# Attention scores of a diffusion step: three products over 64 rows become two products over 128 rows

## The chip, the cores and the metric

The kernel runs on one core of one Trainium2 chip. What is compared is device time in microseconds (us) of one execution of the whole program. The engines in the profile are PE (TensorE, the matmuls), PEld (the weight loads of TensorE, which overlap PE), DVE (VectorE), ACT (ScalarE), POOL (GpSimd) and SP (which here issues most DMAs).

## The reference, cut to what matters

One inference step of a two-layer backbone: layer 0 mixes tokens with a state-space scan, layer 1 with differential attention, and each is followed by a convolutional feed-forward block (FFN). There are 512 latent tokens ("sample") and 128 context tokens ("prompt"), width 1024. The change is in layer 1's attention only: 8 heads, and for each head two key maps of 64 dimensions.

```python
def diff_attend(q, k, v, lam):                       # q: b, lq, heads, 2 maps, 64
    def one_block(qi):                               # 128 queries
        s = jnp.einsum('bqhcd,bkhcd->bhcqk', qi, k) * DA_SCALE
        p = jax.nn.softmax(s, axis=-1)
        w = p[:, :, 0] - lam * p[:, :, 1]
        return jnp.einsum('bhqk,bkhd->bqhd', w, v)
    ...
qs, ks_ = rope_2d(qs, tabs), rope_2d(ks_, tabs)
k_all = jnp.concatenate([cache_k, ks_], axis=1)      # 128 cached + 512 own keys = 640
os_ = diff_out(diff_attend(qs, k_all, v_all, lam), ...)
op = diff_out(diff_attend(qp, kp, vp, lam), ...)     # the prompt sees its own 128 keys only
```

## The kernel before, in words

Activations are kept transposed: 128 channels on the partitions, 640 tokens (512 sample, 128 prompt) along the free dimension. A matmul in full precision is made of three products of `float32r` operands, each operand being split into a high part and a low part (`hi`, `lo`): hi*hi + hi*lo + lo*hi. `float32r` matmuls, weight tile by weight tile, are the dense work (tiles named q, k, v, po, up, ba, bb and so on).

A head's 128 channels hold both key maps: rows 0 to 63 are map 0, rows 64 to 127 are map 1. `attention` (L1299) loops over 8 heads. For each head it runs a q tile and a k tile on PE (8 steps of 6 matmuls each), copies them out of PSUM (`att_evac`, L1168), applies the rotary positions on DVE and splits into high and low parts (`att_q`, L1184: tiles `qh`, `ql`; `att_k`, L1193: `kh`, `kl`, 640 keys), and then adds the generator `att_head` (L1203) as a task. The v tile of the head follows. Tasks are advanced by `hook`, called after every dense step, so that the scores of head h are issued among the dense steps of head h+1; a "tick" is one dense step of six matmuls.

`att_head` first does the prompt (tile `sp`, plain float32, 128 queries by 128 keys, one matmul per map over that map's 64 rows; operands `qp`, `kp`). Then come four blocks b = 0 to 3 of 128 queries. A block takes two PSUM buffers (`sl`, one per map, from the pool `psd` of three buffers, which the dense tiles share), and fills them with 12 matmuls of 64 rows by 320 columns:

```python
for j, (x, kk) in enumerate(((qh, kh), (qh, kl), (ql, kh))):
    for c0 in (0, 320):
        for r, hf in zip(rs, half):      # map 0: rows 0-63, map 1: rows 64-127
            self.mm(r[...], x[hf, qb], kk[hf, c0:c0 + 320], j == 0, j == 2)
```

`softmax` follows for each map: a maximum on DVE (`sm<-sl`, L1212) and an exponential with row sums on ACT (`e<-sl`, L1213), which is the last reader of the PSUM buffer. Two ticks later `combine` makes the weights w of the block. When all four are done, `att_tail` (L1253) transposes the weights (`wt`, five groups of four float32 transposes through the one PSUM bank "m"), splits each group on ACT and DVE (`wTh`, `wTl`) and multiplies with v (`ov`). So the tail of head h-1, the scores of head h and the dense tiles of head h+1 are interleaved on PE.

The order on each engine is set by the framework's scheduler, which knows the order of the program, the dependencies and costs of its own; each engine then runs its own list strictly in order. The scores in the trace from 1062 to 1077 us are head 0's, 1090 to 1113 head 1's, 1131 to 1150 head 2's, then heads 3 to 6 at intervals of about 37.3 us, and 1308 to 1334 head 7's, among the matmuls of the output projection (`po`).

Of the kernel before, what the change touches and what calls it, by code (L numbers as in the profile page):

```python
# [18 lines left out]
P = 128  # L19
D = 1024  # L20
KT = D // P
TP = 128
TS = 512
T = TP + TS
# [3 lines left out]
PO = 256  # L28
# [5 lines left out]
NH = 32  # L34
FH = 2816
FT = FH // P
SUB = (((0, 8), (8, 15), (15, 22)), ((0, 7), (7, 14), (14, 22)))
MID = (9, 8)
DA_SCALE = 64 ** -0.5
# [128 lines left out]
class Step:  # L168
# [539 lines left out]
    def ffn(self, l, h, nextnorm, pool):  # L708
        nc = self.nc
        cw = pool.tile([P, 2 * FT, 4], F32, tag="fcw", name=f"fcw{l}", bufs=1)  # L710
        nc.sync.dma_start(cw, self.a["fcw"][l])
# [40 lines left out]
        blk = Blocks(self, h, epilogue, place)  # L752
        t = cw[:, FT + std:, 0:3]
        nc.vector.tensor_scalar(t, t, -1.0, None, ALU.mult)
        sums = None
        self.start_tiles(h)
        self.weight_sums(l, range(11, 14, SUMS) if l else range(std, FT, SUMS), h[0][0])
        done = 0
        sub = SUB[l]
        for s, (k0, k1) in enumerate(sub):  # L760
            last = s == len(sub) - 1
            self.down = False
            end = min(k1 + 1, FT)
            while done < end:
# [357 lines left out]
    def att_consts(self, pool):  # L1122
        nc, a = self.nc, self.a
        t = lambda shape, name, dt=F32: pool.tile(shape, dt, tag=name, name=name, bufs=1)
        self.rope = t([P, 2, TS], "rope")
        nc.sync.dma_start(self.rope, a["rope"])
        lv = t([P, 256], "lv")
        nc.sync.dma_start(lv, a["lam"])
        ls = t([P, 2], "ls")
        lj = t([P, 64], "lj")  # L1130
        for i in range(2):
            nc.vector.tensor_tensor_reduce(lj, lv[:, 128 * i:128 * i + 64], lv[:, 128 * i + 64:128 * i + 128], 1.0, 0.0,
                                           ALU.mult, ALU.add, ls[:, i:i + 1])
# [34 lines left out]
    def att_evac(self, ps, hd, name, pool):  # L1168

        x = self.slot("f", f"{name}{hd}", bufs=NF)[:, :TS]  # L1170
        p = pool.tile([P, TP], F32, tag=f"{name}p", name=f"{name}p{hd}", bufs=2)
        self.act(x, ps[:, PO:PO + TS], AF.Copy)
        self.act(p, ps[:, PO + TS:PO + T], AF.Copy, scale=DA_SCALE if name == "q" else 1.0)
        return x, p

    def att_rope(self, out, x):
# [7 lines left out]
    def att_q(self, x, hd, pool):  # L1184

        q = self.tmp("q")[:, :TS]
        self.att_rope(q, x)
        hi, lo = (pool.tile([P, TS], F32R, tag=f"q{nm}", name=f"q{nm}_{hd}", bufs=2) for nm in "hl")
        self.act(hi, q, AF.Copy, scale=DA_SCALE)
        self.stt(lo, q, DA_SCALE, hi.bitcast(F32), ALU.mult, ALU.subtract)  # L1190
        return hi, lo

    def att_k(self, x, hd, pool):  # L1193

        k = self.tmp("k")
        self.nc.sync.dma_start(k[:, TS:], self.a["ck"][hd])
        self.att_rope(k[:, :TS], x)
        hi, lo = (pool.tile([P, T], F32R, tag=f"k{nm}", name=f"k{nm}_{hd}", bufs=2) for nm in "hl")
        self.act(hi, k, AF.Copy)
        self.tt(lo, k, hi.bitcast(F32), ALU.subtract)  # L1200
        return hi, lo

    def att_head(self, hd, qp, kp, qs, k, vs, o, pool):  # L1203


        nc = self.nc
        (qh, ql), (kh, kl) = qs, k
        half = [slice(64 * m, 64 * m + 64) for m in range(2)]
# [17 lines left out]
        for m, hf in enumerate(half):  # L1226
            self.mm(r[:, 512 * m:512 * m + TP], qp[hf], kp[hf], True, True)
        st = stats()
        em = [softmax(r[:, 512 * m:512 * m + TP], TP, m, st) for m in range(2)]
        yield 2  # L1230
        last = hd == 7
        w = pool.tile([P, TP], F32, tag="wp", name="wp", bufs=1)
        combine(w, TP, *em, st)
        yield 3 if last else 4
        ws = []
        for b in range(4):
            qb = slice(b * P, (b + 1) * P)
            rs = [self.psd.tile([P, 1024], F32, tag="d", name="sl") for _ in range(2)]
            for j, (x, kk) in enumerate(((qh, kh), (qh, kl), (ql, kh))):
                for c0 in (0, 320):  # L1240
                    for r, hf in zip(rs, half):
                        self.mm(r[:, 192 + c0:192 + c0 + 320], x[hf, qb], kk[hf, c0:c0 + 320], j == 0, j == 2)
            st = stats()
            em = [softmax(r[:, 192:832], T, m, st) for m, r in enumerate(rs)]
            yield 2
            wb = pool.tile([P, T], F32, tag="w", name=f"w{b}", bufs=8)
            combine(wb, T, *em, st)
            ws.append(wb)
            if b < 3:
                yield ((1, 1, 1) if last else (1, 3, 1) if hd else (1, 3, 3))[b]  # L1250
        self.tails[hd] = self.add(self.att_tail(hd, w, ws, vs, o, pool), 1 if last else 2)
# [89 lines left out]
    def weight_units(self):  # L1341
# [10 lines left out]
        def ffn(l):  # L1352
# [10 lines left out]
            out = []  # L1363
            for k0, k1 in SUB[l]:
                end = min(k1 + 1, FT)
# [185 lines left out]
```

## Time and profile before

| what | value |
|---|---|
| time, median of 3 runs | 1862.02 us (1861.01 to 1862.44) |
| the profiled execution itself | 1865.19 us |
| its span, first to last instruction | 1863.4 us |
| busy PE / PEld / DVE / ACT | 1830.9 (98%) / 1715.6 (92%) / 1464.3 (79%) / 998.1 us (54%) |
| mean granted TensorE clock | 0.994 |
| attention stage, first q copy to last head's output | about 1049 to 1359 us |

The span is the time between the first and the last instruction; the 1.8 us around it are launch and end. A group of the profile is a line, an engine, an operation and tile names "out<-in", with shapes as partitions x elements. In a timeline a row is a start, a duration and a run of equal instructions (xN). Matmuls overlap in the pipeline, so a matmul's own duration (0.30 us for 320 columns) is longer than the time until the next may start; what a matmul costs is read from the distance between starts. Some matmul records can be missing.

### The profile page before, as it was taken

The page shows a single profiled execution, that of the slowest core. Times are in us where ns is not written, and L with a number is a line of the kernel's source. Part 1 is how long each engine was busy: PE and PEld are TensorE (multiplying, and loading weights), DVE is VectorE, ACT ScalarE, POOL GpSimd, SP SyncE. Part 2 cuts the span into 40 slices and gives each one's busy share as a digit, 9 for nine tenths or more (in the row PEclk, how much of TensorE's full clock was granted, in tenths as well). Part 3 has the DMA queues.
Part 4 walks back from the last instruction along what each step waited for, and adds up shares of the span by engine and source line. Part 5 has one row for each costly group of instructions (what it writes and reads, how often), then busy time and mean ns, then how long its engine had stood idle before and what let it go on. Part 6 is the DMA issues. An engine that isn't in the chain of part 4 may idle for free.

```text
span 1863.4 us, 33068 instructions
## 1 busy us (share of the span) xinstructions
PE 1830.9 (98%) x13057; PEld 1715.6 (92%) x13057; DVE 1464.3 (79%) x2827; ACT 998.1 (54%) x1862; POOL 55.7 (3%) x84
## 2 busy tenths in 40 slices
PE   7999999999999999999999999999999999999997
PEld 5899999999989999999999988888899999999996
DVE  5689999999848999998586877778779874874874
ACT  3379686879426442244363566566546543643641
POOL 0000000000001100011000000000001011100000
PEclk9999999999999999999999999999999999999998
DMA  9734244445547976677642211111047368853421
GB/s 339 270 108 147 92 126 128 114 132 177 184 148 220 279 217 211 208 205 201 208 133 77 88 46 59 57 52 49 21 129 193 95 180 237 250 166 103 142 80 57
DMA packets 108675, 276.06 MB, mean 148 GB/s; under 512 B 12284, under 2 KB 19048, under 8 KB 102504
## 3 DMA queue, kind: packets, MB, share of 16 engines
q1 hardware_dynamic: 100520, 225.19, 37.4%
q0 software_dynamic: 7424, 48.24, 11.0%
q8 instruction: 102, 1.67, 0.4%
q10 hardware_dynamic: 576, 0.52, 0.1%
q14 instruction: 53, 0.43, 0.1%
HBM read 267.95 MB, written 54.19 MB: 173 GB/s over the span
## 4 chain that ended last, share of the span: by engine, by line
PE 93%; DVE 3%; ACT 2%; DMA 1%; issue 1%; SPq 0%; DVEq 0%; ACTq 0%
PE po L230 25%; PE up L230 14%; PE bb L230 6%; PE ba L230 6%; PE bc L230 6%; PE z L230 6%; PE x L230 5%; PE st L230 5%; PE v L230 3%; PE yp L230 3%; PE q L230 2%; PE sl L230 2%; PE k L230 2%; PE ov L230 2%; PE in L230 1%; PE wt L1275 1%
## 5 line engine op out<-in xcount | busy, mean ns | idle before, releaser
L221 ACT ACTIVATE whi<-raw 128x1024 fp32r<-128x1024 f32 (+4 forms) x266 | 270.9, 1020 | 318.8 <-PE po L230 189.9
L227 DVE TENSOR_TENSOR wlo<-raw,whi 128x1024 fp32r<-128x1024 f32 (+4 forms) x266 | 312.4, 1175 | 79.8 <-ACT whi L221 68.2
L224 DVE SCALAR_TENSOR_TENSOR xr<-po,mod,xr 128x256 f32<-128x256 f32 (+2 forms) x231 | 89.0, 433 | 123.6 <-PE po L230 123.5
L230 PE MATMUL po<-ml,whi 128*128 128x256 f32 (+1 forms) x704 | 168.1, 310 | 0.0
L230 PE MATMUL po<-mh,whi 128*128 128x256 f32 (+1 forms) x704 | 167.8, 310 | 0.0
L230 PE MATMUL po<-mh,wlo 128*128 128x256 f32 (+1 forms) x704 | 167.8, 309 | 0.0
L230 PEld LDWEIGHTS po<-mh,whi 128*128 128x128 f32 x704 | 128.1, 188 | 0.8 <-ACT mh L221 0.5
L230 PEld LDWEIGHTS po<-mh,wlo 128*128 128x128 f32 x704 | 128.7, 188 | 0.0
L230 PEld LDWEIGHTS po<-ml,whi 128*128 128x128 f32 x704 | 128.5, 188 | 0.1
L230 PE MATMUL up<-h01h,wlo 128*128 128x256 f32 x464 | 105.7, 308 | 0.0
L230 PE MATMUL up<-h01l,whi 128*128 128x256 f32 x464 | 105.6, 308 | 0.0
L230 PE MATMUL up<-h01h,whi 128*128 128x256 f32 x464 | 105.6, 308 | 0.0
L230 PEld LDWEIGHTS up<-h01h,whi 128*128 128x128 f32 x464 | 84.4, 188 | 0.0
L230 PEld LDWEIGHTS up<-h01h,wlo 128*128 128x128 f32 x464 | 84.4, 188 | 0.0
L230 PEld LDWEIGHTS up<-h01l,whi 128*128 128x128 f32 x464 | 84.3, 188 | 0.0
L221 ACT ACTIVATE mh<-cv 128x640 fp32r<-128x640 f32 x44 | 32.4, 737 | 88.3 <-DVE cv L227 88.3
L221 ACT ACTIVATE e<-sl,sm 128x640 f32<-128x640 f32 x64 | 50.4, 790 | 40.2 <-DVE sm L1212 39.8
L688 DVE CUSTOM_DVE_ANT_0 junk<-mw,cbc 128x1024 bf16<-128x1024 f32 x48 | 58.5, 1219 | 8.4 <-DMA mw<-in_modT 8.3
L230 PE MATMUL z<-h00h,whi 128*128 128x256 f32 (+1 forms) x256 | 62.9, 325 | 0.0
L221 ACT ACTIVATE ca<-ca 128x640 f32<-128x640 f32 x44 | 32.3, 735 | 55.4 <-DVE ca L224 55.3
L230 PE MATMUL bb<-T,whi 128*128 128x320 f32 x264 | 61.6, 313 | 0.0
L221 ACT ACTIVATE e<-rb,Ctok 128x128 f32<-128x128 f32 x160 | 56.3, 389 | 8.5 <-issue 6.1
(580 smaller groups left out, 5317.5 us busy)
## 6 DMA issues: line engine op xcount, KB each, us to landing
wsum<-in_w_blk POOLq DMA_DIRECT2D x42, 768.0 KB, 7.1
raw<-in_w_blk SPq DMA_DIRECT2D x55, 512.0 KB, 4.0
mw<-in_modT SPq DMA_DIRECT2D x48, 512.0 KB, 4.4
raw<-wsum SPq DMA_DIRECT2D x92, 256.0 KB, 3.0
raw<-in_w_in SPq DMA_DIRECT2D x40, 512.0 KB, 5.4
rb<-rowd SPq DMA_DIRECT2D x40, 512.0 KB, 5.6
raw<-in_w_dn SPq DMA_DIRECT2D x32, 448.0 KB, 3.4
raw<-in_w_qkv SPq DMA_DIRECT2D x24, 512.0 KB, 3.3
```

The lines of the kernel that those rows point to most:

```text
L221: return self.pin(self.nc.scalar.activation(out, in_, func, **k))
L224: return self.pin(self.nc.vector.scalar_tensor_tensor(out, in0, s, in1, op0, op1))
L227: return self.pin(self.nc.vector.tensor_tensor(out, a, b, op))
L230: return self.pin(self.nc.tensor.matmul(out, lhsT, rhs, start=start, stop=stop, **k))
L688: nc.vector.tensor_tensor_reduce(w if c else junk, w, cb[:, c, :], 1.0, 0.0, ALU.mult, ALU.add, self.mod[l][:, t, c:c + 1])
L1275: nc.tensor.transpose(pm[:, b * P:(b + 1) * P], ws[b][:, kc * P:(kc + 1) * P], self.ident)
```

## The change

The three products over 64 rows are written as two products over 128 rows. For map m the key tile `k{m}` now holds the high part of the map's keys in the map's own 64 rows and the low part in the other 64 rows. The query tile `qh{m}` holds the map's high part twice, once in each half, so that one matmul over 128 rows gives hi*hi + hi*lo. A second matmul uses `ql{m}`: the low part in the map's own rows and zeros in the other half; these two tiles exist once for all heads (their zero halves are written once, on ACT, as zero times the rotary table). A block has 8 matmuls of 128 rows by 320 columns instead of 12 of 64 rows. Since PE writes the same two PSUM buffers, softmax and everything behind it are unchanged; the loop over maps is now the outer one.

The prompt scores take `kp` whole (128 rows) and a query tile `qz` with one column block per map, in which the other map's rows are zero (two buffers, kept for all heads, zeroed once on DVE).

The splits become: for q four ACT copies and two DVE subtractions on 64 partitions (before: one and one on 128); for k two and two (before one and one); for the prompt's q two copies (before one). Where a half goes to the other 64 rows, the engine reads one half of the partitions and writes the other.

```diff
+MAPS = [slice(0, 64), slice(64, 128)]
...
+        self.ql = [t([P, TS], f"ql{m}", F32R) for m in range(2)]
+        self.qz = [t([P, 2, TP], f"qz{i}") for i in range(2)]
+        for m, oth in enumerate(MAPS[::-1]):
+            self.act(self.ql[m][oth], self.rope[oth, 0, :], AF.Copy, scale=0.0)
+            for z in self.qz:
+                nc.vector.memset(z[oth, m, :], 0.0)
... att_evac
-        p = pool.tile([P, TP], F32, tag=f"{name}p", name=f"{name}p{hd}", bufs=2)
         self.act(x, ps[:, PO:PO + TS], AF.Copy)
-        self.act(p, ps[:, PO + TS:PO + T], AF.Copy, scale=DA_SCALE if name == "q" else 1.0)
+        if name == "q":
+            p = self.qz[hd % 2]
+            for m, own in enumerate(MAPS):
+                self.act(p[own, m, :], ps[own, PO + TS:PO + T], AF.Copy, scale=DA_SCALE)
+            return x, p
... att_q
-        hi, lo = (pool.tile([P, TS], F32R, tag=f"q{nm}", name=f"q{nm}_{hd}", bufs=2) for nm in "hl")
-        self.act(hi, q, AF.Copy, scale=DA_SCALE)
-        self.stt(lo, q, DA_SCALE, hi.bitcast(F32), ALU.mult, ALU.subtract)
+        hi = [pool.tile([P, TS], F32R, tag=f"qh{m}", name=f"qh{m}_{hd}", bufs=2) for m in range(2)]
+        for m, own in enumerate(MAPS):
+            self.act(hi[m][own], q[own], AF.Copy, scale=DA_SCALE)
+            self.act(hi[m][MAPS[1 - m]], q[own], AF.Copy, scale=DA_SCALE)
+            self.stt(self.ql[m][own], q[own], DA_SCALE, hi[m][own].bitcast(F32), ALU.mult, ALU.subtract)
... att_k
-        self.act(hi, k, AF.Copy)
-        self.tt(lo, k, hi.bitcast(F32), ALU.subtract)
+        for m, own in enumerate(MAPS):
+            self.act(hl[m][own], k[own], AF.Copy)
+            self.tt(hl[m][MAPS[1 - m]], k[own], hl[m][own].bitcast(F32), ALU.subtract)
... att_head
-            self.mm(r[:, 512 * m:512 * m + TP], qp[hf], kp[hf], True, True)
+            self.mm(r[:, 512 * m:512 * m + TP], qp[:, m, :], kp, True, True)
...
-            for j, (x, kk) in enumerate(((qh, kh), (qh, kl), (ql, kh))):
-                for c0 in (0, 320):
-                    for r, hf in zip(rs, half):
-                        self.mm(r[:, 192 + c0:192 + c0 + 320], x[hf, qb], kk[hf, c0:c0 + 320], j == 0, j == 2)
+            for m, r in enumerate(rs):
+                for j, x in enumerate((qs[m], self.ql[m])):
+                    for c0 in (0, 320):
+                        self.mm(r[:, 192 + c0:192 + c0 + 320], x[:, qb], k[m][:, c0:c0 + 320], j == 0, j == 1)
```

How the scheduler's lists change is seen at three places. The first is PE at block 0 of head 3, among the tail of head 2 (`wt`, `ov`). Before, from the block's second piece up to the transposes that part it from its last (kh and kl are the key parts, qh and ql the query parts):

```order
L230 MATMUL sl<-kh_12972,qh_12961 128x320 x2
L230 MATMUL ov<-wTh,vh_12686 128x512
L230 MATMUL sl<-kh_12972,qh_12961 128x320
L230 MATMUL sl<-kl_12973,qh_12961 128x320 x3
L1275 MATMUL wt<-cst,w_12756 128x128
```

After, the whole block (k_3 and qh_3 with the lower number are map 0's tiles, with the higher number map 1's; ql the same):

```order
L231 MATMUL sl<-k_3_12956,qh_3_12941 128x320 x2
L231 MATMUL sl<-k_3_12956,ql_11546 128x320 x2
L231 MATMUL ov<-wTh,vh_12682 128x512
L231 MATMUL sl<-k_3_12957,qh_3_12942 128x320 x2
L231 MATMUL sl<-k_3_12957,ql_11547 128x320 x2
L1288 MATMUL wt<-cst,w_12748 128x128
```

Before, the block's 12 matmuls stand in four pieces of 1, 2, 4 and 5, with two groups of transposes and five v products between them; after, its 8 matmuls stand in two pieces of 4 with one v product between.

The second place is PE at block 3 of head 3, among the k tile of head 4. Before:

```order
L230 MATMUL k<-h10h_11394,wlo_13101 128x384
L230 MATMUL sl<-kh_12972,qh_12961 128x320 x2
L230 MATMUL sl<-kl_12973,qh_12961 128x320 x2
L230 MATMUL sl<-kh_12972,ql_12962 128x320
L230 MATMUL sl<-kh_12972,qh_12961 128x320 x2
L230 MATMUL sl<-kl_12973,qh_12961 128x320 x2
L230 MATMUL sl<-kh_12972,ql_12962 128x320 x3
L230 MATMUL k<-h10h_11396,whi_13100 128x256
```

After:

```order
L231 MATMUL k<-h10h_11394,wlo_13087 128x384
L231 MATMUL sl<-k_3_12956,qh_3_12941 128x320 x2
L231 MATMUL sl<-k_3_12956,ql_11546 128x320 x2
L231 MATMUL sl<-k_3_12957,qh_3_12942 128x320 x2
L231 MATMUL sl<-k_3_12957,ql_11547 128x320 x2
L231 MATMUL k<-h10h_11396,whi_13086 128x256
```

Before, the scheduler put five matmuls of one map ahead of the other map's first (the two maps' PSUM buffers come free one after the other), so that the two halves of the rows are not issued in turn; after, one map follows the other as the program has it. The block stands between the same dense steps of the k tile.

The third place is ACT at the split of q for head 3. Before:

```order
L221 ACTIVATE e_12879,sm<-sl,sm 128x640
L221 ACTIVATE qh_12961<-q 128x512
L221 ACTIVATE e_12879<-e_12879,sm 128x640
L221 ACTIVATE e_12920,sm<-sl,sm 128x640
L221 ACTIVATE e_12923,sm<-sl,sm 128x640
```

After:

```order
L222 ACTIVATE kp_12932<-k 128x128
L222 ACTIVATE qh_3_12941<-q 64x512 x2
L222 ACTIVATE qh_3_12942<-q 64x512 x2
L222 ACTIVATE wpT<-wpt 128x128
L222 ACTIVATE wTh<-wt 128x512
L222 ACTIVATE k_3_12956<-k 64x640
L222 ACTIVATE k_3_12957<-k 64x640
```

The q copy stood among the exponentials of block 2 of the head before; the four copies now stand behind the last exponential of block 3.

More of the change, by code (lines that the diff above doesn't have):

```diff
@@ L1170, in att_evac @@
         x = self.slot("f", f"{name}{hd}", bufs=NF)[:, :TS]
-        p = pool.tile([P, TP], F32, tag=f"{name}p", name=f"{name}p{hd}", bufs=2)
         self.act(x, ps[:, PO:PO + TS], AF.Copy)
-        self.act(p, ps[:, PO + TS:PO + T], AF.Copy, scale=DA_SCALE if name == "q" else 1.0)
+        if name == "q":
[3 more added lines that the diff above has]
+            return x, p
+        p = pool.tile([P, TP], F32, tag="kp", name=f"kp{hd}", bufs=2)
+        self.act(p, ps[:, PO + TS:PO + T], AF.Copy)
         return x, p
@@ L1187, in att_q @@
         self.att_rope(q, x)
-        hi, lo = (pool.tile([P, TS], F32R, tag=f"q{nm}", name=f"q{nm}_{hd}", bufs=2) for nm in "hl")
-        self.act(hi, q, AF.Copy, scale=DA_SCALE)
-        self.stt(lo, q, DA_SCALE, hi.bitcast(F32), ALU.mult, ALU.subtract)
-        return hi, lo
+        hi = [pool.tile([P, TS], F32R, tag=f"qh{m}", name=f"qh{m}_{hd}", bufs=2) for m in range(2)]
[3 more added lines that the diff above has]
+            self.stt(self.ql[m][own], q[own], DA_SCALE, hi[m][own].bitcast(F32), ALU.mult, ALU.subtract)
+        return hi
     def att_k(self, x, hd, pool):
@@ L1197, in att_k @@
         self.att_rope(k[:, :TS], x)
-        hi, lo = (pool.tile([P, T], F32R, tag=f"k{nm}", name=f"k{nm}_{hd}", bufs=2) for nm in "hl")
-        self.act(hi, k, AF.Copy)
-        self.tt(lo, k, hi.bitcast(F32), ALU.subtract)
-        return hi, lo
+        hl = [pool.tile([P, T], F32R, tag=f"k{m}", name=f"k{m}_{hd}", bufs=2) for m in range(2)]
+        for m, own in enumerate(MAPS):
+            self.act(hl[m][own], k[own], AF.Copy)
+            self.tt(hl[m][MAPS[1 - m]], k[own], hl[m][own].bitcast(F32), ALU.subtract)
+        return hl
     def att_head(self, hd, qp, kp, qs, k, vs, o, pool):
         nc = self.nc
-        (qh, ql), (kh, kl) = qs, k
-        half = [slice(64 * m, 64 * m + 64) for m in range(2)]
         def softmax(s, n, m, st):
@@ L1225, in att_head @@
         r = self.psd.tile([P, 1024], F32, tag="d", name="sp")
-        for m, hf in enumerate(half):
-            self.mm(r[:, 512 * m:512 * m + TP], qp[hf], kp[hf], True, True)
+        for m in range(2):
+            self.mm(r[:, 512 * m:512 * m + TP], qp[:, m, :], kp, True, True)
         st = stats()
```

## The prediction

> **What bounds the kernel now.** I read the page first, then busy time by stage, then the waits of the attention stage, then PE's own timeline there.
>
> ```profile
> span 1863.4 us, 33068 instructions
> PE 1830.9 (98%) x13057; PEld 1715.6 (92%) x13057; DVE 1464.3 (79%) x2827; ACT 998.1 (54%) x1862; POOL 55.7 (3%) x84
> ```
>
> PE is the bound of the whole. The change touches only the stage of the attention heads, so I look at one head's period (from the first matmul of a q tile to that of the next; columns: length, then busy time of PE, PEld, DVE, ACT, POOL):
>
> ```profile
> 1127.40:1162.94 35.54, 35.54 (x247) 31.64 (x246) 28.00 (x57) 22.02 (x47) 0.00 (x0) 1.00 0.19 60
> 1162.94:1200.22 37.28, 37.25 (x248) 32.11 (x248) 28.30 (x57) 22.28 (x49) 0.00 (x0) 1.00 0.17 58
> 1237.52:1274.80 37.28, 37.26 (x248) 32.08 (x248) 28.32 (x57) 22.28 (x49) 0.00 (x0) 1.00 0.15 47
> ```
>
> The heads from the third on repeat: 37.28 us with PE never idle, at full clock, DVE idle for 9.0 us and ACT for 15.0. The period that holds head 2's scores does the same work in 35.54. What PE's time consists of is seen in the scores. The two rows of the waits (whole stage; total us, times, longest) say that weight loads of the scores often start late:
>
> ```profile
> PEld sl L230 <- issue: 9.6, 35, 0.5
> PEld sl L230 <- ACT e L221: 3.8, 14, 0.8
> ```
>
> Now PE's timeline of head 3, block 0 (start, duration, operation):
>
> ```profile
> 1164.93 0.46 PE L230 MATMUL q<-h10h,wlo 128*128 128x256 f32 x2
> 1165.32 0.41 PE L230 MATMUL sl<-kh,qh 64*128 64x320 f32 x1
> 1165.66 0.66 PE L1275 MATMUL wt<-cst,w 128*128 128x128 f32 x4
> ...
> 1166.39 0.40 PE L230 MATMUL ov<-wTh,vl 128*128 128x512 f32 x1
> 1166.71 0.41 PE L230 MATMUL sl<-kh,qh 64*128 64x320 f32 x2
> 1167.06 0.50 PE L230 MATMUL ov<-wTh,vh 128*128 128x512 f32 x1
> 1167.49 0.56 PE L230 MATMUL sl<-kl,qh 64*128 64x320 f32 x3
> 1167.98 0.66 PE L1275 MATMUL wt<-cst,w 128*128 128x128 f32 x4
> ...
> 1169.03 0.70 PE L230 MATMUL sl<-kh,ql 64*128 64x320 f32 x4
> 1169.66 0.56 PE L230 MATMUL q<-h10h,whi 128*128 128x256 f32 x2
> ```
>
> Four visits, each counted from its start to the next row: 0.34 + 0.35 + 0.49 + 0.63 = 1.81 us. Block 1 is one visit:
>
> ```profile
> 1173.92 0.56 PE L230 MATMUL sl<-kh,qh 64*128 64x320 f32 x4
> 1174.32 0.45 PE L230 MATMUL sl<-kl,qh 64*128 64x320 f32 x4
> 1174.61 0.45 PE L230 MATMUL sl<-kh,ql 64*128 64x320 f32 x4
> 1174.99 0.33 PE L1164 MATMUL vt<-cst,v 128*128 128x128 f32 x1
> ```
>
> 1.07 us, and in its middle four matmuls take 0.29: the two maps, on different halves of the rows, run side by side. Blocks 2 and 3, with the ACT rows that free their second PSUM buffer:
>
> ```profile
> 1180.27 0.55 PE L230 MATMUL sl<-kh,qh 64*128 64x320 f32 x2
> 1180.47 0.27 ACT L221 ACTIVATE qp<-q 128x128 f32<-128x128 f32 x1
> 1180.79 0.41 PE L230 MATMUL sl<-kh,qh 64*128 64x320 f32 x1
> 1181.86 0.56 PE L230 MATMUL k<-h10h,whi 128*128 128x256 f32 x2
> ...
> 1184.61 0.79 ACT L221 ACTIVATE e<-sl,sm 128x640 f32<-128x640 f32 x1
> 1184.76 0.56 PE L230 MATMUL sl<-kh,qh 64*128 64x320 f32 x2
> 1185.54 0.56 PE L230 MATMUL sl<-kh,qh 64*128 64x320 f32 x2
> 1186.61 0.56 PE L230 MATMUL k<-h10h,whi 128*128 128x256 f32 x2
> 1187.01 0.46 PE L230 MATMUL k<-h10l,whi 128*128 128x256 f32 x2
> ```
>
> 1.59 and 1.85 us for the same 12 matmuls. The second map starts only when its buffer is free (copy done at 1180.74, exponential at 1185.40), the first map's matmuls run alone meanwhile, and the pairing is lost.
>
> The price of a matmul as the change writes it stands in the FFN, which runs 128 rows by 320 columns in the same type:
>
> ```profile
> 1727.20 0.46 PE L230 MATMUL ba<-T,whi 128*128 128x320 f32 x2
> ...
> 1731.88 0.31 PE L230 MATMUL ba<-h11h,whi 128*128 128x320 f32 x1
> ```
>
> Between these two starts lie 32 matmuls: 4.68 / 32 = 0.146 us each, 0.293 for two.
>
> **The change, step by step.** *Scores, before.* Head 3's visits sum to 1.81 + 1.07 + 1.59 + 1.85 = 6.32 us. Around them lies more. A pair of dense matmuls has the 640 columns of two of the FFN's, so 0.293; the pair ahead of block 0 takes 0.39 (1164.93 to 1165.32), the one behind block 3 0.40 (1186.61 to 1187.01). So entering costs about 0.10 and leaving 0.11: with seven visits, of which four leave to float32r work, 0.7 + 0.44 = 1.14 us. In all 7.46 us a head.
>
> *Scores, after.* 4 blocks x 8 matmuls x 0.146 = 4.68 us. If the edges come from changing between 64 and 128 rows, they vanish; I leave 0.13 for edges to the float32 transposes. The Trainium skill ("TensorEngine Tiling (Array Packing)", Key Properties) says that a change of tiling mode drains TensorE. By that rule the edges go; the rows of 0.39 and 0.40 agree with it, and by its opposite (edges stay, 1.14) the head would save 1.64 where I count 2.65 (7.46 - 4.68 - 0.13).
>
> Against the change speaks another rule of the Trainium skill ("TensorE: Matmul & The Clock Gate", Part 3: Packing small matmuls): matmuls on different row groups run together, and one with few rows takes as long as one with all. By it a block has 6 slots before and 8 after, 0.29 us more, and the sum would be +9.4 us for 32 blocks. Block 1's middle row (four in 0.29) agrees; blocks 0, 2 and 3, with 1.81, 1.59 and 1.85 where six slots would be 0.88, do not.
>
> *New waits at blocks 2 and 3.* The buffers come free as before. In block 2 the q copy is followed by two prompt copies instead of one, so the buffer is free 0.27 later, at 1181.0 on before's clock; PE wants it at 1180.2 + 0.59 = 1180.8: about 0.25 lost. In block 3 PE wants the second buffer at about 1184.85. The exponential ended at 1185.40; in the new list DVE does the rotary shuffle behind block 2's maxima instead of ahead (a 512-column DVE operation, 0.67 like ql below, less a short row of the norm's chain that stays between: I estimate 0.4 us gained), so 0.15 to 0.2 lost. Together 0.45: a steady head saves 2.65 - 0.45 = 2.2 us. Bounds: 2.8 (no waits, no edges) and -1.2 (the rule's 8 slots).
>
> *Splits.* They are priced by the rows of the whole tile and, for 64 partitions, by one ACT row of layer 0:
>
> ```profile
> L221 ACT ACTIVATE qh<-q x8: 614/631/632, 1055.6 to 1298.0; 128x512 fp32r<-128x512 f32 x8
> L224 DVE SCALAR_TENSOR_TENSOR ql<-q,qh x8: 667/671/691, 1056.5 to 1301.2; 128x512 fp32r<-128x512 f32 x8
> L221 ACT ACTIVATE kh<-k x8: 722/732/739, 1057.8 to 1306.2; 128x640 fp32r<-128x640 f32 x8
> L227 DVE TENSOR_TENSOR kl<-k,kh x8: 818/824/827, 1058.6 to 1307.3; 128x640 fp32r<-128x640 f32 x8
> L221 ACT ACTIVATE dtraw<-in,dtb 64x640 f32<-64x640 f32 x1 | 0.8, 775 | 0.0
> ```
>
> 640 columns on 64 partitions cost ACT 0.78 us, on 128 0.73: half the partitions save nothing. So a head adds three q copies (1.89), one k copy (0.73) and one prompt copy (0.27) on ACT, 2.9 us, and 0.67 + 0.82 = 1.5 us on DVE. Cover: in a period of 35.1 us DVE has 29.8 of work and ACT 25.2, so 5.3 and 9.9 idle. The q copies now stand behind block 3's last exponential and ahead of the tail's first wTh; the next head's scores, which need them, start 16 us after block 3 ends (one period after this head's: 1165.32 + 37.28 = 1202.60, against 1186.61). I take nothing beyond the 0.45; if the cover were gone, at most 4.4 a head. DVE's subtractions write the one pair of ql tiles, after the scores of the head before, and nothing else on DVE waits for them.
>
> *Prompt scores.* Two matmuls over 128 rows instead of two side by side, with edges saved: nothing, within 0.2 a head. *Setup*: four memsets and two ACT copies of 0.6 once, while PE has its q and k tiles ahead: nothing, at most 1.2. Sample and prompt DMAs are the same and pass each other by a place on SP: nothing.
>
> *Heads that differ.* Heads 1 and 3 to 6: 5 x 2.2 = 11.0. Head 2's block 0 was unbroken, 1.74 shorter: 0.5. Head 0 and head 7 wait for softmax:
>
> ```profile
> 1070.00:1100.00 30.00, 29.31 (x166) 24.88 (x164) 19.18 (x38) 17.79 (x38) 0.00 (x0) 0.89 0.13 39
> 1075.29 0.90 PE L230 MATMUL sl<-kh,qh 64*128 64x320 f32 x2 [0.58 <-ACT e L221]
> ```
>
> There PE waits for exponentials, and the granted clock falls to 0.89. The chain of maxima and exponentials stays, part of head 1's q copies joins it, PE gains little: 1 us for each of the two heads (between 3 lost and 4 gained).
>
> The sum: 11.0 + 0.5 + 2.0 = 13.5 us. The profiled execution took 1865.19, 3.2 above the median of 1862.02; from the median, 1848.5 us.
>
> **The rivals.** *Rows were the resource (slower).* In all 32 blocks two slots more at 0.146: +9.4 us, 1871. It decides if a block and its edges take more than 7.46 / 4 = 1.87 us, that is if the edges and the late second map are waits that stay. For it: block 1 and the 14 waits put down to the exponential. Against: edges stand also where nothing is awaited ("issue", 35 times).
>
> *ACT and DVE take PE's place (no change).* 4.4 us more a head on two engines that run strictly in order, at DVE 85% of the period. If two thirds of the 2.2 go into waits of blocks 2, 3 and of the tail's ov for wTh, some 3 us are left: 1859; if all and the first head's chain grows by 3, 1865. For it: both second buffers already came just in time. Against: 5.3 us of idle DVE in a period.
>
> *No waits at all.* 5 x 2.8 + 1.5 + 3 + 3 = 21.5: 1840.5. For it: softmax starts earlier too, since map 0 is finished first.
>
> **How the numbers follow.** The forecast (1842 to 1856) has 0.66, no waits 0.08, ACT and DVE 0.19 (of it 0.05 still faster, 0.09 the same, 0.05 slower), rows 0.07. 0.2%, or 3.7 us, is about what this measurement can tell from no change: faster 0.79, same 0.09, slower 0.12. The range 1840 to 1860 leaves out the rows, half of the second rival and the best of no waits, 0.2 in all.
>
> **What would show it.** Right: scores in PE's timeline at 0.146 from start to start, dense pairs beside them at 0.29, periods of about 35.1 us, PE without idle in them. Wrong: PE rows of block 2 and 3 waiting for ACT for more than 0.5 us; starts of 0.2 or more within a map; periods of 37 us with DVE above 80%; a longer stretch of clock below 1 around head 0.

## The result and the profile after

| | median | range, runs | profiled execution | its span |
|---|---|---|---|---|
| before | 1862.44 us | 1861.01 to 1864.92, 5 | 1865.19 us | 1863.4 us |
| after | 1845.53 us | 1843.33 to 1846.46, 5 | 1845.76 us | 1844.0 us |

The ratio is 0.9903 (95% interval 0.9891 to 0.9914). That is 16.9 us less; 13.5 were predicted. The page of after begins:

```profile
span 1844.0 us, 32868 instructions
...
PE 1806.3 (98%) x12929; PEld 1711.7 (93%) x12929; DVE 1477.7 (80%) x2847; ACT 1022.8 (55%) x1904; POOL 56.9 (3%) x84
```

PE runs 128 matmuls fewer and is busy 24.6 us less, DVE 13.4 and ACT 24.7 us more. The periods that hold the scores of heads 2, 3 and 5 (columns as before):

```profile
1121.82:1155.61 33.79, 33.43 (x226) 31.17 (x225) 28.76 (x59) 23.84 (x52) 0.00 (x0) 1.00 0.26 79
1155.61:1190.59 34.98, 34.81 (x234) 32.38 (x234) 30.56 (x62) 26.30 (x56) 0.00 (x0) 1.00 0.14 46
1225.12:1260.08 34.96, 34.77 (x233) 32.37 (x233) 30.52 (x62) 26.26 (x56) 0.00 (x0) 1.00 0.13 39
```

37.28 has become 34.98 (and 34.53 for head 4). The predicted 35.1 stands there. Block 0 of head 3 in PE's timeline, then blocks 2 and 3 with the ACT rows that free their second PSUM buffer, and the first maximum of block 2 (`sm<-sl`):

```profile
1158.54 0.45 PE L231 MATMUL sl<-k,qh 128*128 128x320 f32 x2
1158.83 0.45 PE L231 MATMUL sl<-k,ql 128*128 128x320 f32 x2
1159.12 0.40 PE L231 MATMUL ov<-wTh,vh 128*128 128x512 f32 x1
1159.36 0.46 PE L231 MATMUL sl<-k,qh 128*128 128x320 f32 x2
1159.66 0.45 PE L231 MATMUL sl<-k,ql 128*128 128x320 f32 x2
1159.95 0.60 PE L1288 MATMUL wt<-cst,w 128*128 128x128 f32 x4
...
1172.01 0.58 ACT L222 ACTIVATE q<-q 128x512 f32<-128x512 f32 x1
1172.49 0.54 ACT L222 ACTIVATE qz<-q 64x128 f32<-64x128 f32 x2
...
1172.81 0.46 PE L231 MATMUL sl<-k,qh 128*128 128x320 f32 x2
1173.11 0.46 PE L231 MATMUL sl<-k,ql 128*128 128x320 f32 x2
1173.40 0.46 PE L231 MATMUL sl<-k,qh 128*128 128x320 f32 x2
1173.60 0.82 DVE L1225 TENSOR_REDUCE sm<-sl 128x1 f32<-128x640 f32 x1
1173.70 0.46 PE L231 MATMUL sl<-k,ql 128*128 128x320 f32 x2
1173.99 0.46 PE L231 MATMUL k<-h10h,whi 128*128 128x256 f32 x2
1174.29 0.47 PE L231 MATMUL k<-h10l,whi 128*128 128x256 f32 x2
1174.46 0.80 ACT L222 ACTIVATE e<-sl,sm 128x640 f32<-128x640 f32 x1 [1.43 <-DVE sm L1225]
...
1175.42 0.80 ACT L222 ACTIVATE e<-sl,sm 128x640 f32<-128x640 f32 x1
...
1176.65 0.46 PE L231 MATMUL sl<-k,qh 128*128 128x320 f32 x2
...
1177.24 0.46 PE L231 MATMUL sl<-k,qh 128*128 128x320 f32 x2
```

Every pair of matmuls takes 0.29 to 0.30, inside a block and beside it (1173.99 to 1174.29: the dense pair behind the scores, 0.40 before). Block 2 takes 1.18 us in place of 1.59. Nothing waits: block 2's second buffer is free at 1173.03 and wanted at 1173.40, block 3's at 1176.22 and wanted at 1177.24.

Where the time of the attention stage went is told in three stretches: A, the periods with the scores of heads 0 to 2; B, those of heads 3 to 5; C, from there to the start of the last row of `ov` or `op` matmuls (the end of head 6, and head 7 among `po`). Single periods at the start are not compared, since groups of the tail move from one to the next. Both kernels were profiled a second time among the experiments.

| us | A | B | C | sum |
|---|---|---|---|---|
| before | 110.52 | 111.88 | 76.74 | 299.14 |
| before, second profile | 107.72 | 111.80 | 78.21 | 297.73 |
| after | 103.90 | 104.47 | 71.44 | 279.81 |
| after, second profile | 104.12 | 104.42 | 71.47 | 280.01 |

### The profile page after: what moved, and what is told of

Its sections match the earlier page's. It is cut to its first block, busy times and chain, and to the rows that moved or that the text cites. A ratio compares the mean times of both kernels' runs of the same rounds, so it can differ in the third digit from the quotient of the medians.

```text
span 1844.0 us, 32868 instructions
## 1 busy us (share of the span) xinstructions
PE 1806.3 (98%) x12929; PEld 1711.7 (93%) x12929; DVE 1477.7 (80%) x2847; ACT 1022.8 (55%) x1904; POOL 56.9 (3%) x84
## 3 DMA queue, kind: packets, MB, share of 16 engines
q8 instruction: 101, 1.65, 0.4%
## 4 chain that ended last, share of the span: by engine, by line
PE 91%; ACT 3%; DVE 3%; DMA 1%; issue 1%; SPq 0%; DVEq 0%; ACTq 0%
PE po L231 25%; PE up L231 14%; PE bb L231 7%; PE z L231 6%; PE ba L231 6%; PE bc L231 6%; PE x L231 5%; PE st L231 5%; PE yp L231 3%; PE q L231 2%; PE ov L231 2%; PE sl L231 2%; PE k L231 1%; PE in L231 1%; PE v L231 1%; ACT qh L222 1%
```

## The experiments

One table first; the ratio is to the runs of before in the same set, "steady" is the mean period of heads 3 to 5, and "scores" PE's time in it from a score matmul's start to the next row's.

| run | what it is | median us | ratio (95% interval) | steady | scores | A | B | C |
|---|---|---|---|---|---|---|---|---|
| x6_one_half | before, both maps on one row half | 1879.55 | 1.0088 (1.0073 to 1.0103) | 39.25 | 8.39 | 114.82 | 117.74 | 82.32 |
| before | | 1862.44 | 1 | 37.29 | 6.32 | 110.52 | 111.88 | 76.74 |
| x1_64_mapouter | before, maps outermost | 1857.14 | 0.9961 (0.9947 to 0.9976) | 36.61 | 5.89 | 110.91 | 109.82 | 72.16 |
| z3_before_ticks | before, blocks 2 and 3 later | 1866.09 | 1.0027 (1.0015 to 1.0038) | 37.71 | 4.71 | 111.65 | 113.14 | 73.25 |
| x2_128_12 | 128 rows, still 12 matmuls | 1854.95 | 0.9951 (0.9936 to 0.9966) | 36.48 | 7.07 | 108.47 | 109.43 | 71.97 |
| x3_maps_inner | after, maps innermost | 1848.28 | 0.9913 (0.9899 to 0.9928) | 35.57 | 4.89 | 104.49 | 106.71 | 72.51 |
| after | | 1845.53 | 0.9903 (0.9891 to 0.9914) | 34.82 | 4.84 | 103.90 | 104.47 | 71.44 |
| z0_after_again | after once more | 1844.18 | 0.9904 (0.9888 to 0.9919) | 34.81 | 4.85 | 104.12 | 104.42 | 71.47 |
| z4_after_ticks | after, blocks 2 and 3 later | 1851.26 | 0.9945 (0.9932 to 0.9957) | 35.30 | 4.80 | 106.58 | 105.90 | 72.16 |
| x7_prompt_old | after, prompt as before | 1844.26 | 0.9905 (0.9887 to 0.9922) | 34.81 | 4.83 | 103.31 | 104.43 | 71.47 |
| y1_dup_dma | after, doubled parts by DMA | 1843.95 | 0.9894 (0.9879 to 0.9909) | 34.64 | 4.82 | 103.48 | 103.92 | 71.14 |
| y2_dup_pool | after, doubled parts on POOL | 1849.15 | 0.9925 (0.9911 to 0.9940) | 35.28 | 4.83 | 105.99 | 105.85 | 72.05 |
| x5_128_oldsplits | after, splits of before | 1841.54 | 0.9882 (0.9865 to 0.9898) | 34.85 | 4.96 | 101.90 | 104.55 | 70.04 |

The stretches are those of one execution, and in some of these the granted clock is 0.50 for 3.41 or 6.83 us, which costs half of that. It lies in A for before (6.83), x6, x3 and z3 (3.41 each), in B for z3 (3.41), and in C for before (3.41; 6.83 in its second profile) and x6 (6.83). The other profiles have none in A, B or C.

**Do the two halves run side by side, and what was it worth?** One edit in before:

```diff
-                        self.mm(..., x[hf, qb], kk[hf, c0:c0 + 320], j == 0, j == 2)
+                        self.mm(..., x[:64, qb], kk[:64, c0:c0 + 320], j == 0, j == 2)
```

> The kernel before, in its own order, but both maps read rows 0 to 63 of kh, kl, qh and ql, so that no two matmuls of a block lie on different halves of the rows. Leaves out map 1's own operands (both maps get map 0's scores). Theory (side-by-side running of the two halves is real, and it was worth what lies between 12 slots and the visits seen): a block that stands in one piece takes 12 x 0.146 = 1.75 us and not 1.07 (block 1) or 1.59 (block 2); some 0.7 to 1.1 us a head, so 5 to 9 us slower than before: 1868 to 1873. Rival (halves don't matter, every matmul goes one after another anyway): block 1 stays at 1.07 and the time at 1863.

16 us slower. PE's list is that of before, and block 1 of head 3 now reads:

```profile
1178.84 0.85 PE L230 MATMUL sl<-kh,qh 64*128 64x320 f32 x4
1179.53 0.74 PE L230 MATMUL sl<-kl,qh 64*128 64x320 f32 x4
1180.11 0.75 PE L230 MATMUL sl<-kh,ql 64*128 64x320 f32 x4
1180.79 0.33 PE L1164 MATMUL vt<-cst,v 128*128 128x128 f32 x1
```

1.95 us where it was 1.07, and the whole head 1.96 more. So side-by-side running was real in before and worth 2 us a head, though three of four blocks had lost part of it; I had expected 0.7 to 1.1. A matmul of half the rows took as long as one of all rows: in the middle of the block four take 0.58 us (1179.53 to 1180.11), 0.145 each against 0.146.

**Rows or order?** First the loops of before alone, then full rows with the products of before:

```diff
 x1_64_mapouter
-            for j, (x, kk) in enumerate(((qh, kh), (qh, kl), (ql, kh))):
-                for c0 in (0, 320):
-                    for r, hf in zip(rs, half):
+            for r, hf in zip(rs, half):
+                for j, (x, kk) in enumerate(((qh, kh), (qh, kl), (ql, kh))):
+                    for c0 in (0, 320):
 x2_128_12: maps outermost too; hi[m], lo[m] are tiles with zeros in the other half
+                        self.mm(..., x[m][:, qb], kk[:, c0:c0 + 320], j == 0, j == 2)
...
+        hi, lo = self.qhz[hd % 2], self.qlz
+        for m, own in enumerate(MAPS):
+            self.act(hi[m][own], q[own], AF.Copy, scale=DA_SCALE)
+            self.stt(lo[m][own], q[own], DA_SCALE, hi[m][own].bitcast(F32), ALU.mult, ALU.subtract)
```

> The kernel before with one edit: the loop over the two maps is the outer one, so that the 12 matmuls of 64 rows of a block run map by map and never side by side. Theory (a 64-row float32r matmul that runs alone takes the slot of a full one, 0.146 us, and a change between 64 and 128 rows costs 0.10 us on the way in and 0.11 on the way out): 12 x 0.146 = 1.75 us a block, with one visit a block 1.96 with its edges, 7.8 us a head against 7.46 before, so 0 to 4 us slower than before (1862 to 1866), with dense pairs of 0.39 to 0.40 still standing beside the scores. Rival 1 (side-by-side running was what counted, 6 slots a block): 8 heads x 4 blocks x 6 x 0.146 = 28 us slower, 1890. Rival 2 (what counted was that map 0 is finished early, so that softmax starts early): most of the gain is here already, 1848 to 1852.

> Full rows without fewer products: the three products of before, each over 128 rows, with one q tile per map and part whose other half is zero (kh and kl as before, maps outermost, 12 matmuls of 128 rows a block). Theory: 48 x 0.146 = 7.0 us a head, the edges beside the scores are gone (dense pairs of 0.29), so 0.84 us a head below the first run of this set (64 rows, maps outermost), some 6.7 us in all: 1857 to 1861, and 16 x 0.146 = 2.3 us a head above the changed kernel. Rival (edges are not from the rows but from the late weight loads of the scores): dense pairs of 0.39 to 0.40 stay beside the scores and the time is that of the first run. Rival 2 (the gain came from maps outermost): 1848.

x1 missed: it is 6.6 us faster than before. Block 2 of head 3 shows why:

```profile
1175.31 0.55 PE L230 MATMUL sl<-kh,qh 64*128 64x320 f32 x2
1175.71 0.30 PE L230 MATMUL sl<-kl,qh 64*128 64x320 f32 x1
1175.71 0.41 PE L230 MATMUL sl<-kh,qh 64*128 64x320 f32 x1
...
1176.78 0.56 PE L230 MATMUL k<-h10h,whi 128*128 128x256 f32 x2
1177.18 0.45 PE L230 MATMUL k<-h10l,whi 128*128 128x256 f32 x2
```

In the list all six matmuls of map 0 stand ahead of map 1's first. Yet a kh,qh matmul, which can only be map 1's, starts at 1175.71, when three of map 0 have started (the third of them at the same 1175.71) and three have not: the block takes 1.47, not 1.75. So PE does not keep its list strictly, as was said ahead of the prediction, where two matmuls use different halves of the rows. Besides, with this loop the scheduler writes every block of heads 2 to 6 in one piece. The edges are still there (1176.78 to 1177.18: 0.40). x2 missed too: 1854.95 lies below the expected 1857 to 1861, and the step from x1 is 2.2 us and not 6.7 (x1's blocks had taken 1.47 and not 1.75), with intervals that overlap. Its rows do tell the edges. Block 2 and what follows:

```profile
1176.68 0.46 PE L231 MATMUL sl<-kh,qh 128*128 128x320 f32 x2
...
1178.45 0.46 PE L231 MATMUL k<-h10h,whi 128*128 128x256 f32 x2
1178.74 0.47 PE L231 MATMUL k<-h10l,whi 128*128 128x256 f32 x2
```

12 matmuls in 1.77 and the dense pair at 0.29. So the edges belong to the change between 64 and 128 rows: x2's scores take 1.18 us a head more than x1's, and the rest of the period 1.31 less. From x2 to after, 16 matmuls a head go: scores 7.07 to 4.84, the period 36.48 to 34.82. With 9 us by the two ratios it is the largest single step; from before to x1 it is 7, from x1 to x2 some 2.

**Could before have had it without more rows?** Two numbers of `att_head`, in before (z3) and in after (z4):

```diff
-                yield ((1, 1, 1) if last else (1, 3, 1) if hd else (1, 3, 3))[b]
+                yield ((1, 1, 1) if last else (1, 4, 2) if hd else (1, 3, 3))[b]
```

> The kernel before with two numbers changed: the pauses after the blocks of a head, (1, 3, 1) ticks, are (1, 4, 2), so that blocks 2 and 3 come a tick or two later, when the PSUM buffer of their second map is free; the scheduler then writes all 12 matmuls of most blocks in one piece with the two maps alternating. Products, rows and splits are those of before. Theory (before lost its time because block 0 stood in four pieces and the second maps of blocks 2 and 3 came late, and not because of its 64 rows as such): each block takes about 1.07 us, as block 1 does, and 0.21 for the edges, 5.4 us a head instead of 7.46: 1.5 to 2 us in each of heads 2 to 6, 8 to 10 us in all, 1851 to 1856. Rival (64 rows cost by themselves; one has to use all 128): less than 3 us, 1860 or more.

> The changed kernel with the same two numbers, (1, 4, 2). Theory: its second maps don't wait, and its pieces cost no edges, so there is nothing left to win in the scores: within 2 us of 1845.5. Rival (the pieces of block 0 and the tail's order cost something here too): 3 us or more faster.

Both theories missed in the total (z4 is 5.7 us above 1845.5). z3 has the time that its rival gave, 1860 or more, but not for the rival's reason: its scores did what the theory expected. Block 2 of its head 3, and PE some 5 us later:

```profile
1181.09 0.56 PE L230 MATMUL sl<-kh,qh 64*128 64x320 f32 x4
1181.49 0.45 PE L230 MATMUL sl<-kl,qh 64*128 64x320 f32 x4
1181.78 0.45 PE L230 MATMUL sl<-kh,ql 64*128 64x320 f32 x4
1182.17 0.56 PE L230 MATMUL k<-h10h,whi 128*128 128x256 f32 x2
...
1187.96 0.27 PE L1258 MATMUL wpt<-cst,wp 128*128 128x128 f32 x1
1190.31 0.56 PE L230 MATMUL v<-h10h,whi 128*128 128x256 f32 x2 [2.08 <-ACT e L221]
```

1.08 us for a block of 12, the head's scores 4.71 in place of 6.32, as short as in after. The gain was given back in a new wait: block 3 now stands so late that the v tile behind it finds its PSUM buffer still held by block 3's exponential. That costs 2.3 us a head (2.35 from the `wpt` row to the next), and z3 is slower than before. Part of this is the clock: in its profile half clock stands behind such a wait in head 5's period, and without the 1.7 us lost there the steady period is 37.1 and not 37.71. z4 pays 1.2 us a head at the same place and gains nothing in its scores. So a 64-row block that runs paired is as cheap as the new one but for its edges (1.08 + 0.21 against 1.18); what this pause does to the tail decides. No run pairs every block of before without moving block 3, so how much more than x1's 6.6 us an order alone could have had stays open.

**Is the early end of map 0 the gain?** In after, the map loop innermost again:

```diff
-            for m, r in enumerate(rs):
-                for j, x in enumerate((qs[m], self.ql[m])):
-                    for c0 in (0, 320):
+            for j in range(2):
+                for c0 in (0, 320):
+                    for m, r in enumerate(rs):
+                        x = (qs[m], self.ql[m])[j]
```

> The changed kernel with one edit: the loop over the maps is innermost, as it was before the change; the same 8 matmuls of 128 rows a block in another order, so that both maps are finished together and the second PSUM buffer is wanted 0.15 us after the first one instead of 0.59. Theory (the gain is matmul slots and edges; the early end of map 0 only keeps blocks 2 and 3 from waiting): waits of 0.1 to 0.4 us at blocks 2 and 3 and a softmax later by 0.44 us, so 0 to 4 us slower than the changed kernel: 1845 to 1850. Rival (the early softmax carries the gain): 1855 or more.

1848.28: as the first theory has it, some 2 us slower than after by the ratios, though their intervals overlap, and the scores alike (4.89). Its period is 0.75 us longer a head; the extra in A is less than the 1.7 us that half clock costs there. The order of the maps isn't what carries the change.

**What do the splits cost?** x5 takes them back and keeps PE's matmuls; y1 and y2 move the two doubled copies away from ACT; x7 takes back the prompt's part.

```diff
 x5_128_oldsplits: q, and k likewise
-        for m, own in enumerate(MAPS):
-            self.act(hi[m][own], q[own], AF.Copy, scale=DA_SCALE)
-            self.act(hi[m][MAPS[1 - m]], q[own], AF.Copy, scale=DA_SCALE)
-            self.stt(self.ql[m][own], q[own], DA_SCALE, hi[m][own].bitcast(F32), ALU.mult, ALU.subtract)
+        self.act(hi, q, AF.Copy, scale=DA_SCALE)
+        self.stt(lo, q, DA_SCALE, hi.bitcast(F32), ALU.mult, ALU.subtract)
 y1_dup_dma
-            self.act(hi[m][MAPS[1 - m]], q[own], AF.Copy, scale=DA_SCALE)
+            self.nc.sync.dma_start(hi[m][MAPS[1 - m]].bitcast(F32), hi[m][own].bitcast(F32))
 y2_dup_pool
+            self.nc.gpsimd.tensor_copy(hi[m][MAPS[1 - m]], hi[m][own])
 x7_prompt_old
-            self.mm(r[:, 512 * m:512 * m + TP], qp[:, m, :], kp, True, True)
+            self.mm(r[:, 512 * m:512 * m + TP], qp[hf], kp[hf], True, True)
```

> The changed kernel's 8 matmuls of 128 rows a block, but with the splits of before: one ACT copy and one DVE subtraction on 128 partitions for q and for k, no doubled high part, no zeros; both maps multiply the same tiles. Leaves out the operands' right places, so its scores are other numbers; PE's work is the same. It prices the 2.6 us of ACT and 1.5 us of DVE that the splits add to a head. Theory (splits are covered but for the tail, where PE waits 0.3 to 0.45 us a head for w and wTh): 2 to 4 us faster than the changed kernel, 1842 to 1844. Rival 1 (fully covered): within 1 us of 1845.5. Rival 2 (they cost PE their own time): 4.1 us a head, 1815.

> The changed kernel with the two doubled high parts of q per head made by a DMA from one half of the tile to the other (SP's queue) in place of an ACT copy: ACT has 1.26 us less in a head. The last set showed that the splits cost nothing in the steady heads (periods 34.85 with the splits of before against 34.82) and 3.6 us in the first head. Theory: the first head gets back the part of its chain that the two copies hold, 1 to 2 us, the other heads nothing: 1843 to 1845. Rival (a DMA comes later than a copy, or waits behind weight transfers on SP's queue, and the first head's scores wait for it): 1847 or more.

> The same two doubled parts made by a copy on POOL, which has nothing else in this stage. Theory: as with the DMA, 1 to 2 us in the first head: 1843 to 1845, if POOL's copy of 64 x 512 takes no longer than about 2 us. Rival (POOL's copies slow DVE's operations beside them, and DVE is 85% busy): DVE operations longer by some tenths, periods above 35 us, 1847 or more.

> The changed kernel with the prompt's scores as before the change: two matmuls of 64 rows, one copy of the prompt's q, no zeros for it. Theory: the prompt's scores take 0.43 us a head in place of 0.36, and leaving 64 rows costs the next dense pair 0.1 more; one ACT copy of 0.27 less: 0 to 2 us slower than the changed kernel, 1845 to 1848. Rival (the added prompt copy holds the PSUM buffer that block 2's second map waits for): 2 us or more faster.

x5 is 4.0 us below after by the medians (the intervals of the ratios overlap a little), half a us under the expected range; by the stretches 2.0 in A, nothing in B, 1.4 in C. So the splits are free where the heads repeat, the tail that the theory named included, and cost 3.4 us where the first and the last head's softmax stands open. x5 also gives the low part of q two buffers, where after has one pair of `ql` tiles, so that its price is in the 3.4 too. (The 3.6 us for the first head in the expectations came from single periods and took in tail groups that had moved.) y1 lies 1.6 us below after, in the expected range, but with intervals that overlap: not told apart. The 1 to 2 us expected in the first head don't show (A is 103.48, after's 103.90 and 104.12). x7 (1844.26, expected 1845 to 1848) is after within the measurement: its scores of the prompt take 0.42 a head and not 0.36, and no buffer waits for the copy. y2 is slower, and the groups between 1052 and 1330 us show by what (after, then y2):

```profile
L225 DVE SCALAR_TENSOR_TENSOR ql<-q,qh 64x512 fp32r<-64x512 f32 x16 | 10.9, 682 | 0.6 <-ACT qh L222 0.5
```

```profile
L1203 POOL CAST qh<-qh 64x512 fp32r<-64x512 f32 x16 | 16.2, 1012 | 373.9 <-ACT qh L222 304.9 <-DVE ru L1191 68.7
L225 DVE SCALAR_TENSOR_TENSOR ql<-q,qh 64x512 fp32r<-64x512 f32 x16 | 14.4, 898 | 0.4 <-ACT qh L222 0.3
```

The copy takes 1.01 us on POOL (0.63 on ACT), and DVE's subtraction beside it goes from 0.68 to 0.90 in the mean. The Trainium skill ("GPSIMD Engine Reference", Specifications) has POOL and DVE contend for SBUF where a DVE instruction reads two SBUF inputs, as this one does: the rows agree.

**The clock.** Both kernels unchanged, for second profiles.

> The kernel before once more, for a second profile: whether the two stretches of low clock (1074 to 1082 us at 0.50, and 1.7 us lost at 1330 to 1340) are there again. If they are, 5.1 us of the difference between the two kernels are the clock's; if not, the profile of before was of a longer execution, which agrees with its 1865.19 us against a median of 1862.44.

> The changed kernel once more, beside the others of this set, for a second profile: whether the granted clock stays at 1.00 around the first and the last head, where it was 0.50 for some 7 us in the profile of before. If the clock there is a property of the changed kernel, it is 1.00 again; if it is a matter of the execution, it may drop.

The granted clock stands ahead of the DMA share. Before, then its second profile:

```profile
1070.00:1080.00 10.00, 9.31 (x44) 7.88 (x43) 7.85 (x17) 8.05 (x18) 0.00 (x0) 0.74 0.03 8
1080.00:1090.00 10.00, 10.00 (x63) 9.21 (x62) 6.45 (x13) 5.29 (x11) 0.00 (x0) 0.92 0.18 53
...
1330.00:1340.00 10.00, 10.00 (x68) 8.80 (x67) 7.43 (x20) 4.93 (x10) 0.00 (x0) 0.83 0.12 41
```

```profile
1070.00:1080.00 10.00, 9.30 (x59) 7.88 (x59) 8.68 (x19) 7.84 (x17) 0.00 (x0) 1.00 0.06 13
...
1320.00:1330.00 10.00, 8.20 (x49) 6.08 (x47) 6.53 (x15) 5.89 (x12) 0.00 (x0) 0.77 0.07 21
1330.00:1340.00 10.00, 10.00 (x63) 9.30 (x60) 8.02 (x17) 4.60 (x9) 0.00 (x0) 0.89 0.09 33
```

At the first head the low clock is a matter of the execution: it cost (0.26 + 0.08) x 10 = 3.4 us once and nothing the second time, with PE busy as long. At head 7 both profiles of before have it, 1.7 and 3.4 us, and x6, with the same list, too; the two of after don't. In before PE stands there twice:

```profile
1327.67 0.33 PE L1164 MATMUL vt<-cst,v 128*128 128x128 f32 x1 [0.58 <-ACT o L221]
1329.21 0.56 PE L230 MATMUL po<-o0h,whi 128*128 128x256 f32 x2 [1.22 <-ACT e L221]
```

After has its waits there cut into pieces of 0.5 and less. But at the first head after waits longer, 1.5 us in one piece (PE is busy for 8.14 of the 10 us from 1070), and keeps its clock in both profiles.

The other traces tell more. All stretches of the granted clock in the middle of these 14 profiles are multiples of 3.41 us, so each profile can be cut into windows of 3.41 us that begin where its clock may change. In the window just ahead of the half clock at head 7 PE is idle for 1.5 us in before (1327.36 to 1330.77, busy for 1.89 of 3.41), 1.8 in its second profile and 1.8 in x6. Half clock also stands behind two windows with 2.1 us idle in z3 (at 1114.8 and 1265.0 us), and behind one with 2.5 in x3 and in z4 (at 1340.3 and 1342.1, after C). From 1040 to 1400 us no window with 1.8 or more goes without it; of nine with 1.45 to 1.7, after's 1.46 among them, two are followed by it. So at head 7 it goes with how PE's waits fall together, and not with the rows: x3 and z4 multiply full rows and lose 1.7 us just behind the stage, x1 multiplies half rows and loses nothing. The first head of before and of x6 does not fit, with 0.2 and 0.4 us idle in the window ahead; what decides there is open.

The Trainium skill ("TensorE: Matmul & The Clock Gate", Part 1) describes a window of activity that runs freely, of about 3.4 us. The multiples of 3.41 us agree with it, and so does that the same wait is followed by half clock in one execution and not in the other.

## Why the prediction was right, point by point

**The steady heads.** Predicted 2.2 us a head, measured 37.29 - 34.82 = 2.47. PE's time in the mean period of heads 3 to 5, from start to start:

| us | scores | q and k | v | wt | ov | sp | other |
|---|---|---|---|---|---|---|---|
| before | 6.32 | 15.49 | 7.50 | 2.03 | 4.46 | 0.42 | 1.08 |
| after | 4.84 | 14.58 | 7.83 | 1.83 | 4.31 | 0.36 | 1.08 |

The step "visits and edges" (7.46 to 4.81, 2.65) was right in kind, and its sum is right to the digit by luck: the scores gave 1.48 where 6.32 - 4.68 = 1.64 was counted, and q, k, `wt` and `sp` gave 0.91 + 0.20 + 0.06 = 1.17 where the edges stood for 1.14 - 0.13 = 1.01. That the 0.91 and 0.20 are edges is read from the pairs that took 0.39 to 0.40 and now take 0.29; the 0.06 are the prompt's own matmuls (0.42 again in x7). The Trainium skill ("TensorEngine Tiling (Array Packing)", Key Properties) has a change of tiling mode drain TensorE. By that rule the edges had to go; x1 and x2 agree, 0.40 against 0.29 behind the scores.

**The waits at blocks 2 and 3** were the step that failed: I took 0.45, and there are none. Head 3's block 2 starts at 1180.27 before and at 1172.81 after. The rows of before follow; those of after (1172.01, 1173.60 and 1174.46) stand with the result:

```profile
1179.99 0.58 ACT L221 ACTIVATE q<-q 128x512 f32<-128x512 f32 x1
...
1182.96 1.55 DVE L1212 TENSOR_REDUCE sm<-sl 128x1 f32<-128x640 f32 x2
...
1183.82 0.80 ACT L221 ACTIVATE e<-sl,sm 128x640 f32<-128x640 f32 x1 [3.08 <-DVE sm L1212]
```

For block 2 I kept before's distance between the q copy and the block and added a copy. The q copy now starts 0.80 us ahead of the block and not 0.28, so the buffer is free in time all the same. For block 3 I let the exponentials of block 2 come 0.4 us earlier. They come 1.9 earlier: the maxima start 0.79 us after the block where it was 2.69, because not only the shuffle has left their way, as predicted, but `w` too (it is now done before the block starts), and the first exponential starts after 1.65 us (1172.81 to 1174.46) where it was 3.55 (1180.27 to 1183.82). Over the periods of heads 3 to 5 ACT's exponentials wait 6.1 us for the maxima, where it was 21.0.

That the rival "no waits at all" had right; what it would have won more was lost in the tail, where v takes 0.33 more and `ov` 0.15 less: 2.65 - 0.18 = 2.47. That 2.2 came so near is two misses of opposite sign, the waits and the tail. One such place in head 3 of after, where the next row should follow after 0.39:

```profile
1184.00 0.87 DVE L225 SCALAR_TENSOR_TENSOR w<-e,sm,e 128x640 f32<-128x640 f32 x1
...
1184.47 0.53 PE L231 MATMUL v<-h10h,whi 128*128 128x256 f32 x2
...
1185.15 0.66 PE L1288 MATMUL wt<-cst,w 128*128 128x128 f32 x4
```

PE reaches the transposes 0.68 after the v row, when w has been ready for 0.28. With the splits of before (x5) v takes 7.60, but q and k 14.94, so that the period is the same; the splits are not shown to be the cause, which stays open.

**The other heads.** Summed as the stretches have it, the prediction was 1 + 2.2 + 0.5 = 3.7 for A, 6.6 for B and 2.2 + 1 = 3.2 for C. Measured between the first profiles: 6.6, 7.4 and 5.3; between the second: 3.6, 7.4 and 6.7. Without the low clock of before (3.4 in A; 1.7 and 3.4 in C) it is 3.2 and 3.6 in A, 3.6 and 3.3 in C. So the 13.5 hold without the clock (14.2 and 14.3), and what the result has beyond that, 2.6 us, is about what the clock around head 7 cost in the two profiles of before. I had seen the low clock only at the first head and had given it no term; two profiles of each kernel are few for its share in the medians.

**The splits** I put at nothing. For the steady heads that is what x5 shows; in A and C they cost 3.4 us, inside the bounds that I gave for the first and last heads. The prompt's part at nothing: x7 agrees.

**The rivals.** "Rows were the resource" had the mechanism right, as x6 and z3 show: paired, 64 rows need 6 slots and not 12 (1.08 us a block in z3, 1.95 in x6). The Trainium skill ("TensorE: Matmul & The Clock Gate", Part 3: Packing small matmuls) has matmuls on different row groups run concurrently; these rows agree. It decided nothing, because before got its pairs whole in one block of four only; had every block been paired and nothing else moved, 0.11 us a block would have been left to win (1.29 with edges against 1.18), 3.5 us in all by this estimate. "ACT and DVE take PE's place" did not come: DVE is busy 30.56 of 34.98 us in the longest period, and the period still got shorter.

## What to carry to other kernels

Count slots in the trace, not in the program: two half-row matmuls shared a slot in full only where the list alternates them and both output buffers are free (1.07 us a block; 1.47 map by map, 1.59 and 1.85 with a late buffer), and each visit with another row count cost 0.2 us on top (0.10 in, 0.11 out). Full-row products with zeros or doubled parts took the same time in either order that was tried (4.84 and 4.89 us of scores a head), where the 64-row ones on two halves took 4.71 to 6.32. A better order and full rows (before to x2) gave as much as the fewer matmuls behind them (x2 to after), 9 us each. When a wait is moved away by delaying a step, look at who takes the buffer next: the same delay gave before's scores 1.6 us a head and lost 2.3 behind them.

## What the runs showed of the hardware that I had not expected

- A 64-row matmul started ahead of three others that stand before it in PE's list and use the other half of the rows (x1, 1175.71). The same 12 take 1.95 us in one half (x6), 1.47 map by map in two halves (x1), 1.07 alternating (before).
- The granted clock changed in steps of 3.41 us, and far shorter waits than that brought it down: every window of 3.41 us with 1.8 us or more of PE idle was followed by half clock (1040 to 1400 us, 14 profiles), after's with 1.46 was not.
- A copy on POOL made the DVE subtraction beside it a third longer (0.68 to 0.90 us).
